# Experts sorted by the quarters of 64 tokens that pick them, and the V product summed in three phases

## The chip, the cores and the metric

The kernel runs on one core of a Trainium2 chip. The metric is the device time of one execution in microseconds; lower is better. The engines are named as in the profile: PE is TensorE (matrix products; PEld its weight loads), DVE is VectorE, ACT is ScalarE, POOL is GpSimd, SP is SyncE, which here only issues transfers.

## What is computed

One decoder layer over 256 tokens of width 2048: a mixer of two attention groups, and after it PEER, a retrieval over 128 x 128 single-neuron experts. Only PEER is touched here:

```python
def peer(xn, wq, subkeys, u, v):
    q = (xt @ wq).reshape(T, PEER_HEADS, 2, PEER_QDIM // 2)
    s1 = einsum('thd,nd->thn', q[:, :, 0], subkeys[0])      # 8 heads, 128 keys on either side
    s2 = einsum('thd,nd->thn', q[:, :, 1], subkeys[1])
    v1, i1 = top_k(s1, 16); v2, i2 = top_k(s2, 16)
    cand = v1[..., :, None] + v2[..., None, :]
    sc, ci = top_k(cand, 16)                                # 16 experts per head: 128 picks per token
    idx = i1[ci // 16] * 128 + i2[ci % 16]
    gate = softmax(sc)
    h = gelu(einsum('cd,chkd->chk', xc, u[ic]))             # xc, ic, gc: 128 tokens at a time
    return einsum('chk,chkd->cd', gc * h, v[ic])            # 16384 experts, rows of 2048
```

The result is `rmsnorm(h + peer(rmsnorm(h)))`, in float32.

## The kernel before

The kernel does not gather the experts of each token. It computes the hidden value of every expert for every token (the U stage), multiplies by the gates (zero where a token has not picked the expert), and multiplies the result A, experts x tokens, by V (the V stage). An expert that no token has picked adds nothing, so the V stage reads only picked experts, in tiles of 128 gathered rows.

**Marks.** While the picks are routed, matmuls of one-hot rows count them into `pc[t]`, one 128x128 table (expert = row and column) for each set `t` of 128 tokens. `used[:, t]` is 1 where a count is over 0.5. The last two columns of experts (`LATE = 2`) are left out of the lists: they are always multiplied, for both sets.

**Lists.** In the second part of the U stage, `todo` holds small steps, one after each `u_block` of 128 experts (`FETCH = 104` is the block by which all must be done). `alone` marks the experts that only set 0, or only set 1, has picked. For each of the two, `turned_sums` and `ranks` count (three small matmuls) the rank of each expert, and `keep` gives the first `128 * SINGLE` of them a place. The rest, those of both sets and those that did not fit, get places by `keep_rest`. `spots` and 16 `list_run`s turn places into the tables `idxA` and `idxV`, one column for each tile. So there are 27 + 27 tiles with a single set and 50 tiles with both, 104 in all (`LIST`); with the two late ones the V stage has 106. If the last list overflows, a branch at the end (`tc.If`) runs the other 102 tiles; it costs nothing otherwise.

**V stage.** `SEQ` is the order of the tiles: the two late ones, then a both-tile followed by one or two single ones, 48 times, then two both-tiles. For tile `n`:

- `gather_v` (line 1045, POOL) gathers 128 rows of V, 8 KB each, into one of 7 places of `ring`; it is called 6 tiles ahead.
- `gather_a` (line 1049, POOL) gathers 128 rows of `At` (256 tokens, 1 KB) into one of 3 buffers `ar`, 3 tiles ahead.
- `v_parts` (lines 1107 and 1108) splits each half of the V rows (128x1024) into a rounded part `hi` (ACT) and a remainder `lo` (DVE). There are four buffers of each, enough for two tiles.
- `a_parts` (lines 1096 and 1097) does the same with A: `ah` (ACT) and `al` (DVE), two buffers each. For a single tile only 128 tokens are split.
- `v_products` (lines 1143 to 1145) does three matmuls for each of four column blocks `c` of 512 and for each set `t` that the tile has: 12 for a single tile, 24 for a both-tile. They add into the eight PSUM banks `sums[t, c]`, from the first tile to the last. Six of the banks have the name `pv` in the profile, and the two with `t = 1, c > 1` are called `mm`.

The parts of tile `i + 1` are issued, with high priority, before the products of tile `i`. At the end `finish` (line 1152) adds a bank to `acc`, which holds the residual, and the last norm follows. The order of the instructions on each engine is set ahead of the run by the framework's scheduler, which follows priorities and its own estimate of when things are ready; on the chip every engine runs its list in order and waits on semaphores.

Of the kernel before, what the change touches and what calls it, by code (L numbers as in the profile page):

```python
# [10 lines left out]
F32 = mybir.dt.float32  # L11
F32R = mybir.dt.float32r
F16 = mybir.dt.float16
# [14 lines left out]
BIG = 3e38  # L28
RING = 7
LEAD = 13  # L30
SINGLE = 27
BOTH = 50
LIST = 2 * SINGLE + BOTH
LATE = 2
CAND = [16 // (i + 1) for i in range(16)]
NCAND = sum(CAND)
# [11 lines left out]
def decoder_trunk(ctx, tc, xT, g1, g2, gf, w_cols, w_v, w_out, w_q, u, v, subk, posk, posv,  # L48
# [4 lines left out]
    def f(ap):  # L53
        return ap.bitcast(F32)
# [561 lines left out]
    with ExitStack() as p3:  # L616
# [4 lines left out]
        used = qs0.bitcast(F16)[:, 0:256].rearrange("p (t c) -> p t c", t=2)  # L621

        HU = []

# [30 lines left out]
        with ExitStack() as pr:  # L655
            rt = pr.enter_context(tc.tile_pool(name="rt", bufs=1))
            ps4 = pr.enter_context(tc.tile_pool(name="ps4", bufs=1, space=bass.MemoryType.PSUM))

            pc = [ps4.tile([128, 128], F32, name=f"pc{t}") for t in range(2)]
# [44 lines left out]
            def route(t):  # L704
# [79 lines left out]
                def tok(t0):  # L784
                    if t0 % TG == 0:
                        st["stg"] = rt.tile([128, 128, TG], F32, name="stg", bufs=2)
                    stg = st["stg"]
                    r = t0 // RUN

                    hot = rt.tile([128, 2, RUN // 2, 128, 2], F16, name="hot", bufs=2)  # L790
                    o1 = rt.tile([128, 2, RUN // 2, 128, 2], F16, name="o1", bufs=2)
                    full = [128, RUN, 128, 2]
                    dve.tensor_tensor(hot.rearrange("p a b i j -> p (a b) i j"), iotar[:, None].to_broadcast(full),
                                      iT[:, r].rearrange("p a (b j) -> p (a b) j", j=2)[:, :, None, :].to_broadcast(full),
                                      op=OP.is_equal)
                    half = [128, RUN // 2, 128, 2]
                    for j in range(2):
                        g_ = gT[:, r, j].rearrange("p (b j) -> p b j", j=2)
                        dve.tensor_tensor(o1[:, j], hot[:, 0], g_[:, :, None, :].to_broadcast(half), op=OP.mult)

                    def later():

                        first = None
                        for k0 in range(RUN - 4, -1, -4):
                            pg = ps4.tile([128, 4, 128], F32, name="tp", bufs=4)
                            for k in range(3, -1, -1):
                                for j in (1, 0):
# [5 lines left out]
                                pe.matmul(pc[t], hot[:, 1, (k0 + k) // 2, :, k % 2], hot[:, 0, (k0 + k) // 2, :, k % 2],  # L813
                                          start=c % 128 == RUN - 1, stop=c % 128 == 128 - RUN)
# [46 lines left out]
                settle(1)  # L861
            settle()
            u_end()
            for t in range(2):
                dve.tensor_scalar(used[:, t], pc[t], 0.5, None, op0=OP.is_gt)
            dve.memset(used[:, :, NKEY - LATE:], 0.0)


# [49 lines left out]
        colsum = kp.tile([128, 3], F32, name="colsum")  # L918
        one = [kp.tile([128, 128], F16, name=f"one{t}") for t in range(2)]
        kept = [kp.tile([128, 128], F16, name=f"kept{t}") for t in range(2)]  # L920
        rest = kp.tile([128, 128], F16, name="rest")
        place = kp.tile([128, 128], F32, name="place")
        st2 = {}

        def scratch():
            return psl.tile([128, 512], F32, name="sl", bufs=2)
# [15 lines left out]
            dve.memset(row, 0.0)  # L942
            sp.dma_start(At[0].rearrange("(a b) -> a b", a=2), row[0:2])

        def alone():
            both = up.tile([128, 128], F16, name="both", tag="fT")
            dve.tensor_tensor(both, used[:, 0], used[:, 1], op=OP.mult)
            for t in range(2):
                dve.tensor_tensor(one[t], used[:, t], both, op=OP.subtract)

        def turned_sums(f_, k):
            ps = scratch()
# [14 lines left out]
        def keep(t):  # L967
            ps = ranks(one[t])
            dve.scalar_tensor_tensor(kept[t], ps, 128.0 * SINGLE, one[t], op0=OP.is_lt, op1=OP.mult)
            dst = place if t == 0 else up.tile([128, 128], F32, name="row", bufs=2)  # L970
            dve.scalar_tensor_tensor(dst, ps, 1.0 + 128 * SINGLE * t, kept[t], op0=OP.add, op1=OP.mult)
            if t:
                dve.tensor_tensor(place, place, dst, op=OP.add)

        def others():
            dve.tensor_tensor(rest, used[:, 0], used[:, 1], op=OP.max)
            for t in range(2):
                dve.tensor_tensor(rest, rest, kept[t], op=OP.subtract)

        def keep_rest():  # L980
            ps = ranks(rest)
            pe.matmul(ps_tot := scratch()[:, 0:2], st2["tot"], ones16[:, 0:2], start=True, stop=True)
            dve.tensor_copy(count, ps_tot[:, 0:1])
            dst = up.tile([128, 128], F32, name="row", bufs=2)
            dve.scalar_tensor_tensor(dst, ps, 1.0 + 256 * SINGLE, rest, op0=OP.add, op1=OP.mult)
# [33 lines left out]

        def indices(pool_, pl):  # L1020

            dve.tensor_copy(idxA, pl)
            row = pool_.tile([128, 128], F32, name="row", bufs=2)
            dve.tensor_scalar(row, pl, -1.0, 0.0, op0=OP.add, op1=OP.max)
            dve.tensor_copy(idxV, row)

        todo = [consts2, alone]
        for t in range(2):
            todo += [lambda t=t: turned_sums(one[t], t), lambda t=t: keep(t)]
        todo += [others, lambda: turned_sums(rest, 2), keep_rest, lambda: spots(up, place)]  # L1030
        pl = psl.tile([128, 128], F32, name="pl")
        owing = []
        for r in range(128 // RUN):
# [12 lines left out]

        def gather_a(n):
            AR[n] = kp.tile([128, T], F32, name="ar", bufs=3)
            pool.indirect_dma_start(AR[n], None, At, bass.IndirectOffsetOnAxis(ap=idxA[:, n:n + 1], axis=0))  # L1049


        SEQ, tiles_of = list(range(-LATE, 0)), {}
        for n in SEQ:
            tiles_of[n] = (0, 1)
        for n in range(LIST):
            tiles_of[n] = (0,) if n < SINGLE else (1,) if n < 2 * SINGLE else (0, 1)
        m = BOTH - 2
        for k in range(m):
            SEQ += [2 * SINGLE + k] + list(range(2 * SINGLE * k // m, 2 * SINGLE * (k + 1) // m))
        SEQ += [LIST - 2, LIST - 1]  # L1060

        weighed = 0
        FETCH = 104
# [26 lines left out]
        def a_parts(n):  # L1090
            ar = AR.pop(n) if n >= 0 else AL[4 + n]
            ah = kp.tile([128, T], F32R, name="ah", bufs=2)
            al = kp.tile([128, T], F32R, name="al", bufs=2)
            ts = tiles_of[n]
            s_ = slice(128 * ts[0], 128 * ts[-1] + 128)
            act.activation(ah[:, s_], ar[:, s_], AF.Copy)  # L1096
            dve.tensor_tensor(al[:, s_], ar[:, s_], f(ah[:, s_]), op=OP.subtract)  # L1097
            return ah, al

        def v_parts(n):  # L1100
# [21 lines left out]
        with ExitStack() as pv_:  # L1122
# [13 lines left out]
            ends = {t: [n for n in SEQ if t in tiles_of[n]] for t in range(2)}  # L1136

            def v_products(n, t, c, ah, al, vv):
                hi, lo = vv[c // 2]
                tl, cl = slice(128 * t, 128 * t + 128), slice(512 * (c % 2), 512 * (c % 2) + 512)  # L1140
                first, last = n == ends[t][0], n == ends[t][-1]
                ps = sums[t, c]
                pe.matmul(ps, ah[:, tl], hi[:, cl], start=first, stop=False)  # L1143
                pe.matmul(ps, ah[:, tl], lo[:, cl], start=False, stop=False)  # L1144
                pe.matmul(ps, al[:, tl], hi[:, cl], start=False, stop=last)  # L1145

            scaled = {}

# [26 lines left out]
            for i, n in enumerate(SEQ):  # L1175
# [148 lines left out]
```

## Time and profile before

| | |
|---|---|
| time, median of 3 runs | 1684.7 us (1684.11 to 1686.45) |
| the profiled execution | 1688.74 us, its span 1686.9 us |
| mean granted clock of PE | 0.994 |
| PE busy | 1665.2 us, 99% of the span |
| DVE, ACT, POOL busy | 1225.2, 931.8, 404.4 us |
| PE products of the V stage | 1230.1 to about 1672 us |
| DMA | 383.22 MB, mean 227 GB/s |

A row of the profile names the line, engine and operation, what it writes and reads by the program's names, and a time in ns or us. In the timeline, the first number is the start in us and the second how long it took; the bracket at the end tells how long the engine had been idle, and on whose end it waited. In a table of stretches, each engine has its busy time and its number of instructions, followed by PE's granted clock, the share of the time that the DMA engines were busy, and GB/s. Matmuls overlap in the pipeline, so a row's duration is longer than the distance from one to the next.

### The profile page before, as it was taken

Reading aid. Unit: us, or ns where it says so; the run is one execution under the profiler, and the core shown is the slowest. Engines: PE = TensorE matmul, PEld = TensorE weight load, DVE = VectorE, ACT = ScalarE, POOL = GpSimd, SP = SyncE. Lnnn points to the kernel's source line nnn. Section 1 sums busy time; section 2 is a strip of 40 time slices with the busy share of each in tenths; the row PEclk is TensorE's granted clock in tenths of the full one; section 3 lists DMA queues with packets and bytes.
Section 4 is the critical chain, followed back from the end, with each engine's and each line's share of the span. In section 5 each row is a group of like instructions: output and inputs, shape, how many; then the busy total and the mean of one; then the engine's idle time right before and its main releaser. Section 6 shows DMA issues by size and latency. Waiting matters only on the chain.

```text
span 1686.9 us, 29563 instructions
## 1 busy us (share of the span) xinstructions
PE 1665.2 (99%) x11304; PEld 1495.1 (89%) x11304; DVE 1225.2 (73%) x2209; ACT 931.8 (55%) x1515; POOL 404.4 (24%) x390
## 2 busy tenths in 40 slices
PE   9999999999999999999999999999999999999996
PEld 8998889999999999999888888888878888888885
DVE  7687876688999985776887776555556666666665
ACT  6587765543445565565444444444455555555555
POOL 0010111100042200000211212111155655556550
PEclk9999999999999999999999999999999999999998
DMA  8444434555555676567999757777577777877771
GB/s 305 167 145 132 132 117 163 176 174 170 171 169 174 216 242 211 194 233 242 345 355 331 240 200 268 264 237 237 180 264 282 284 295 281 296 283 284 288 278 62
DMA packets 136289, 383.22 MB, mean 227 GB/s; under 512 B 12008, under 2 KB 67404, under 8 KB 120140
## 3 DMA queue, kind: packets, MB, share of 16 engines
q1 hardware_dynamic: 116172, 258.55, 46.3%
q0 software_dynamic: 19968, 122.70, 19.5%
q8 instruction: 91, 1.49, 0.3%
q14 instruction: 58, 0.48, 0.1%
HBM read 345.77 MB, written 35.44 MB: 226 GB/s over the span
## 4 chain that ended last, share of the span: by engine, by line
PE 95%; DVE 3%; DMA 1%; ACT 1%; issue 0%; SPq 0%; DVEq 0%; ACTq 0%
PE mm L640 17%; PE mm L156 10%; PE mm L157 10%; PE mm L158 10%; PE mm L641 9%; PE pv L1143 7%; PE pv L1144 6%; PE pv L1145 6%; PE mm L1143 2%; PE mm L1144 2%; PE mm L1145 2%; PE mm L556 2%; PE mm L557 2%; PE mm L558 2%; PE tp L809 2%; PE av L528 1%
## 5 line engine op out<-in xcount | busy, mean ns | idle before, releaser
L107 ACT ACTIVATE hi<-raw 128x1024 fp32r<-128x1024 f32 (+1 forms) x370 | 389.8, 1056 | 408.1 <-PE mm L640 156.2
L108 DVE TENSOR_TENSOR lo<-raw,hi 128x1024 fp32r<-128x1024 f32 (+1 forms) x370 | 460.0, 1245 | 190.7 <-ACT hi L107 189.1
L640 PE MATMUL mm<-X,hi 128*128 128x512 f32 x1216 | 429.0, 395 | 0.5 <-DVE hg L649 0.5
L156 PE MATMUL mm<-X,hi 128*128 128x256 f32 x1424 | 409.9, 288 | 0.0
L158 PE MATMUL mm<-X,lo 128*128 128x256 f32 x1424 | 404.1, 284 | 0.0
L157 PE MATMUL mm<-X,hi 128*128 128x256 f32 x1424 | 404.0, 284 | 0.0
L1108 DVE TENSOR_TENSOR lo<-hg,hi 128x1024 fp32r<-128x1024 f32 x212 | 259.8, 1226 | 120.1 <-ACT hi L1107 115.1
L641 PE MATMUL mm<-X,lo 128*128 128x256 f32 x1216 | 339.5, 279 | 0.0
L1107 ACT ACTIVATE hi<-hg 128x1024 fp32r<-128x1024 f32 x212 | 224.3, 1059 | 114.3 <-PE pv L1145 108.4
L640 PEld LDWEIGHTS mm<-X,hi 128*128 128x128 f32 x1216 | 227.9, 187 | 53.8 <-PE sl L953 0.7
L156 PEld LDWEIGHTS mm<-X,hi 128*128 128x128 f32 x1424 | 271.3, 190 | 4.1 <-issue 3.9
L157 PEld LDWEIGHTS mm<-X,hi 128*128 128x128 f32 x1424 | 269.1, 189 | 0.5 <-issue 0.4
L158 PEld LDWEIGHTS mm<-X,lo 128*128 128x128 f32 x1424 | 268.6, 189 | 1.0 <-DVE lo L108 0.6
L641 PEld LDWEIGHTS mm<-X,lo 128*128 128x128 f32 x1216 | 227.9, 187 | 0.0
L1144 PE MATMUL pv<-lo,ah 128*128 128x512 f32 x474 | 180.5, 395 | 0.0
L1143 PE MATMUL pv<-hi,ah 128*128 128x512 f32 x474 | 172.2, 397 | 1.7 <-ACT ah L1096 1.7
L1145 PE MATMUL pv<-hi,al 128*128 128x512 f32 x474 | 160.9, 395 | 0.0
L1045 POOL DMA_INDIRECT hg<-in_v_dram,idxV x104 | 140.3, 1349 | 61.5 <-DVE lo L1108 36.6
L650 POOL TENSOR_TENSOR hg<-hg,rB 128x256 f32<-128x256 f32 x74 | 69.7, 942 | 347.1 <-DVE hg L649 347.1
L1049 POOL DMA_INDIRECT ar<-At,idxA x104 | 111.4, 1071 | 130.8 <-DVE al L1097 110.3
L1143 PEld LDWEIGHTS pv<-hi,ah 128*128 128x128 f32 x474 | 89.1, 188 | 23.8 <-ACT ah L1096 2.0
L1144 PEld LDWEIGHTS pv<-lo,ah 128*128 128x128 f32 x474 | 89.1, 188 | 21.3
(286 smaller groups left out, 2252.9 us busy)
## 6 DMA issues: line engine op xcount, KB each, us to landing
raw<-in_u_dram SPq DMA_DIRECT2D x256, 512.0 KB, 4.7
raw<-in_w_cols_dram SPq DMA_DIRECT2D x42, 512.0 KB, 4.0
raw<-in_w_out_dram SPq DMA_DIRECT2D x32, 512.0 KB, 4.0
raw<-in_w_q_dram SPq DMA_DIRECT2D x32, 512.0 KB, 3.8
gs<-stg SPq DMA_DIRECT2D x16, 1024.0 KB, 4.8
gt<-gs SPq DMA_DIRECT2D x16, 1024.0 KB, 10.8
At<-a SPq DMA_DIRECT2D x31, 512.0 KB, 6.6
tb<-bd SPq DMA_DIRECT2D x16, 256.0 KB, 3.5
```

The lines of the kernel that those rows point to most:

```text
L107: act.activation(hi[:, :n], raw[:, :n], AF.Copy)
L108: dve.tensor_tensor(lo[:, :n], raw[:, :n], f(hi[:, :n]), op=OP.subtract)
L156: pe.matmul(ps, hi[:, i, :], X[:, db, 0:T], start=db == 0, stop=False)
L157: pe.matmul(ps, hi[:, i, :], X[:, db, T:], start=False, stop=False)
L158: pe.matmul(ps, lo[:, i, :], X[:, db, 0:T], start=False, stop=db == DB - 1)
L640: pe.matmul(ps.rearrange("p a t -> p (a t)"), hi[:, i, :], X[:, db], start=db == 0, stop=False)
L641: pe.matmul(ps[:, 0], lo[:, i, :], X[:, db, 0:T], start=False, stop=db == DB - 1)
L1107: act.activation(hi, r_, AF.Copy)
L1108: dve.tensor_tensor(lo, r_, f(hi), op=OP.subtract)
L1143: pe.matmul(ps, ah[:, tl], hi[:, cl], start=first, stop=False)
L1144: pe.matmul(ps, ah[:, tl], lo[:, cl], start=False, stop=False)
L1145: pe.matmul(ps, al[:, tl], hi[:, cl], start=False, stop=last)
```

## The change

Tokens fall into four quarters of 64. The counts are kept by quarter, and every expert gets a code from 1 to 15, the sum of 1, 2, 4, 8 for the quarters that have picked it. Experts with quarters of one half alone are single as before (27 tiles each). Of those picked from both halves, the ones with exactly two quarters (codes 5, 10, 9, 6) get lists of their own, six tiles each. These experts are single in another order of the quarters: with the order 0, 2, 1, 3 the first set of 128 tokens is quarters 0 and 2, and with 0, 3, 2, 1 it is quarters 0 and 3. An entry of `KINDS` holds the phase, the set, the code (None for a half alone) and the number of tiles. The list for both sets has 26 tiles instead of 50; the number of tiles stays 104.

A PSUM bank has a fixed order of tokens in its 128 partitions, so the V stage runs in three phases, one for each order of `ORDERS`. At the end of the first two, `put` adds each bank to `acc`, in two pieces of 64 partitions, and the next phase starts its sums anew. `a_parts` takes the quarters in the phase's order; in the first two phases it splits a tile for both sets in two pieces. The tiles of the first two lists gather only the half row of `At` that they need. In phase 0 three single tiles go before each both-tile, in phase 1 a both-tile begins and four single ones go before each of the others, and in phase 2 three or four.

```diff
+ORDERS = ((0, 2, 1, 3), (0, 3, 2, 1), (0, 1, 2, 3))
+KINDS = ((2, 0, None, 27), (2, 1, None, 27), (0, 0, 5, 6), (0, 1, 10, 6), (1, 0, 9, 6), (1, 1, 6, 6))
-SINGLE = 27
-BOTH = 50
+HALVES = sum(k[3] for k in KINDS)
+BOTH = 26
...
-            for t in range(2):
-                dve.tensor_scalar(used[:, t], pc[t], 0.5, None, op0=OP.is_gt)
+            for q in range(4):
+                dve.tensor_scalar(used[:, q], pc[q // 2][:, q % 2], 0.5, 2.0 ** q, op0=OP.is_gt, op1=OP.mult)
...
+        def codes():
+            for t in range(2):
+                dve.tensor_tensor(used[:, 2 * t + 1], used[:, 2 * t], used[:, 2 * t + 1], op=OP.add)
+            dve.tensor_tensor(used[:, 0], used[:, 1], used[:, 3], op=OP.add)
+            dve.tensor_scalar(rest, used[:, 0], 0.5, None, op0=OP.is_gt)
+
+        def members(k):
+            one = kp.tile([128, 128], F16, name="one", bufs=2)
+            if KINDS[k][2] is None:
+                dve.scalar_tensor_tensor(one, used[:, 3 - 2 * KINDS[k][1]], 0.5, rest, op0=OP.is_lt, op1=OP.mult)
+            else:
+                dve.tensor_scalar(one, used[:, 0], float(KINDS[k][2]), None, op0=OP.is_equal)
+            st2["one"] = one
+            turned_sums(one, k)
...
+        def keep(k):
+            ps, one, cap = ranks(st2["one"]), st2["one"], KINDS[k][3]
+            kept = kp.tile([128, 128], F16, name="kept", bufs=2)
+            dve.scalar_tensor_tensor(kept, ps, 128.0 * cap, one, op0=OP.is_lt, op1=OP.mult)
+            dst = up.tile([128, 128], F32, name="row", bufs=2) if k else place
+            dve.scalar_tensor_tensor(dst, ps, 1.0 + 128 * FROM[k], kept, op0=OP.add, op1=OP.mult)
+            if k:
+                dve.tensor_tensor(place, place, dst, op=OP.add)
+            dve.tensor_tensor(rest, rest, kept, op=OP.subtract)
...
-            dve.tensor_copy(idxA, pl)
+            n = KINDS[0][3]
+            for t in range(2):
+                dve.tensor_scalar(idxA[:, n * t:n * t + n], pl[:, n * t:n * t + n], 2.0, float(t), op0=OP.mult, op1=OP.add)
+            dve.tensor_copy(idxA[:, 2 * n:], pl[:, 2 * n:])
...
+            if n < 2 * KINDS[0][3]:
+                src, dst = At.rearrange("r (t c) -> (r t) c", t=2), AR[n][:, 128 * sets[n][0]:128 * sets[n][0] + 128]
+            else:
+                src, dst = At, AR[n]
+            pool.indirect_dma_start(dst, None, src, bass.IndirectOffsetOnAxis(ap=idxA[:, n:n + 1], axis=0))
...
-        m = BOTH - 2
-        for k in range(m):
-            SEQ += [2 * SINGLE + k] + list(range(2 * SINGLE * k // m, 2 * SINGLE * (k + 1) // m))
-        SEQ += [LIST - 2, LIST - 1]
+        for ph, m in ((0, 4), (1, 4), (2, BOTH - 10)):
+            h, first = halves[ph], 1 if ph else 0
+            if first:
+                SEQ.append(full.pop(0))
+            m -= first
+            for k in range(m):
+                SEQ += h[len(h) * k // m:len(h) * (k + 1) // m] + [full.pop(0)]
+            if ph == 2:
+                SEQ += full
...
@@ in a_parts @@
+            order = ORDERS[phase[n]]
+            if order == tuple(range(4)):
+                s_ = slice(128 * sets[n][0], 128 * sets[n][-1] + 128)
+                views = [(ar[:, s_], ah[:, s_], al[:, s_])]
+            else:
+                views = []
+                quarters = [x_.rearrange("p (q c) -> p q c", q=4) for x_ in (ar, ah, al)]
+                for t in sets[n]:
+                    x, y = order[2 * t:2 * t + 2]
+                    two = slice(x, y + 1, y - x) if y > x else slice(x, y - 1 if y else None, y - x)
+                    views.append((quarters[0][:, two], quarters[1][:, 2 * t:2 * t + 2], quarters[2][:, 2 * t:2 * t + 2]))
...
+            def put(ph, t, c):
+                for k in range(2):
+                    q = ORDERS[ph][2 * t + k]
+                    s = acc[q // 2][64 * (q % 2):64 * (q % 2) + 64, 512 * c:512 * c + 512]
+                    dve.tensor_tensor(s, sums[t, c][64 * k:64 * k + 64], s, op=OP.add)
...
-                for t in tiles_of[n]:
+                for t in sets[n]:
                     for c in range(4):
                         v_products(n, t, c, ah, al, vv)
+                        if phase[n] < 2 and n == ends[phase[n], t][-1]:
+                            with tc.high_priority():
+                                put(phase[n], t, c)
```

More of the change, by code (lines that the diff above doesn't have):

```diff
@@ L30 @@
 LEAD = 13
-SINGLE = 27
-BOTH = 50
-LIST = 2 * SINGLE + BOTH
+ORDERS = ((0, 2, 1, 3), (0, 3, 2, 1), (0, 1, 2, 3))
+KINDS = ((2, 0, None, 27), (2, 1, None, 27), (0, 0, 5, 6), (0, 1, 10, 6), (1, 0, 9, 6), (1, 1, 6, 6))
+HALVES = sum(k[3] for k in KINDS)
+BOTH = 26
+LIST = HALVES + BOTH
 LATE = 2
@@ L620, in decoder_trunk @@
         HG = {}
-        used = qs0.bitcast(F16)[:, 0:256].rearrange("p (t c) -> p t c", t=2)
+        used = qs0.bitcast(F16).rearrange("p (q c) -> p q c", q=4)
         HU = []
@@ L657, in decoder_trunk @@
             ps4 = pr.enter_context(tc.tile_pool(name="ps4", bufs=1, space=bass.MemoryType.PSUM))
-            pc = [ps4.tile([128, 128], F32, name=f"pc{t}") for t in range(2)]
+            pc = [ps4.tile([128, 2, 128], F32, name=f"pc{t}") for t in range(2)]
             VI = rt.tile([128, 2, 2, PH, 2, 16], F32, name="VI", tag="hot", bufs=2)
@@ L812, in later @@
                                 c = t0 + k0 + k
-                                pe.matmul(pc[t], hot[:, 1, (k0 + k) // 2, :, k % 2], hot[:, 0, (k0 + k) // 2, :, k % 2],
-                                          start=c % 128 == RUN - 1, stop=c % 128 == 128 - RUN)
+                                pe.matmul(pc[t][:, c // 64 % 2], hot[:, 1, (k0 + k) // 2, :, k % 2],
+                                          hot[:, 0, (k0 + k) // 2, :, k % 2],
+                                          start=c % 64 == RUN - 1, stop=c % 64 == 64 - RUN)
                             w = t0 % TG + k0
@@ L917, in decoder_trunk @@
         over = kp.tile([128, 128], F32, name="over")
-        colsum = kp.tile([128, 3], F32, name="colsum")
-        one = [kp.tile([128, 128], F16, name=f"one{t}") for t in range(2)]
-        kept = [kp.tile([128, 128], F16, name=f"kept{t}") for t in range(2)]
+        colsum = kp.tile([128, 1 + len(KINDS)], F32, name="colsum")
         rest = kp.tile([128, 128], F16, name="rest")
@@ L923, in decoder_trunk @@
         st2 = {}
+        FROM = [sum(k[3] for k in KINDS[:i]) for i in range(len(KINDS))]
         def scratch():
@@ L943, in consts2 @@
             sp.dma_start(At[0].rearrange("(a b) -> a b", a=2), row[0:2])
-        def alone():
-            both = up.tile([128, 128], F16, name="both", tag="fT")
-            dve.tensor_tensor(both, used[:, 0], used[:, 1], op=OP.mult)
+        def codes():
             for t in range(2):
-                dve.tensor_tensor(one[t], used[:, t], both, op=OP.subtract)
+                dve.tensor_tensor(used[:, 2 * t + 1], used[:, 2 * t], used[:, 2 * t + 1], op=OP.add)
[9 more added lines that the diff above has]
+            turned_sums(one, k)
         def turned_sums(f_, k):
@@ L965, in ranks @@
             return ps[:, 0:128]
[L967 to L972, printed above, removed]
+        def keep(k):
[5 more added lines that the diff above has]
+            if k:
                 dve.tensor_tensor(place, place, dst, op=OP.add)
[L975 to L978, printed above, removed]
+            dve.tensor_tensor(rest, rest, kept, op=OP.subtract)
         def keep_rest():
@@ L984, in keep_rest @@
             dst = up.tile([128, 128], F32, name="row", bufs=2)
-            dve.scalar_tensor_tensor(dst, ps, 1.0 + 256 * SINGLE, rest, op0=OP.add, op1=OP.mult)
+            dve.scalar_tensor_tensor(dst, ps, 1.0 + 128 * HALVES, rest, op0=OP.add, op1=OP.mult)
             dve.tensor_tensor(place, place, dst, op=OP.add)
@@ L1025, in indices @@
             dve.tensor_copy(idxV, row)
[L1027 to L1030, printed above, removed]
+        todo = [consts2, codes]
+        for k in range(len(KINDS)):
+            todo += [lambda k=k: members(k), lambda k=k: keep(k)]
+        todo += [lambda: turned_sums(rest, len(KINDS)), keep_rest, lambda: spots(up, place)]
         pl = psl.tile([128, 128], F32, name="pl")
@@ L1048, in gather_a @@
             AR[n] = kp.tile([128, T], F32, name="ar", bufs=3)
[L1049 to L1056, printed above, removed]
-        m = BOTH - 2
-        for k in range(m):
-            SEQ += [2 * SINGLE + k] + list(range(2 * SINGLE * k // m, 2 * SINGLE * (k + 1) // m))
-        SEQ += [LIST - 2, LIST - 1]
+            if n < 2 * KINDS[0][3]:
[3 more added lines that the diff above has]
+            pool.indirect_dma_start(dst, None, src, bass.IndirectOffsetOnAxis(ap=idxA[:, n:n + 1], axis=0))
+        sets, phase, halves = {}, {}, {}
+        for k, (ph, st_, _, cap) in enumerate(KINDS):
+            for n in range(FROM[k], FROM[k] + cap):
+                sets[n], phase[n] = (st_,), ph
+        for n in list(range(HALVES, LIST)) + list(range(-LATE, 0)):
+            sets[n] = (0, 1)
+        for ph in range(3):
+            two = [[n for n in range(HALVES) if phase[n] == ph and sets[n] == (t,)] for t in range(2)]
+            halves[ph] = [n for pair in zip(*two) for n in pair]
+        SEQ, full = list(range(-LATE, 0)), list(range(HALVES, LIST))
+        for ph, m in ((0, 4), (1, 4), (2, BOTH - 10)):
[7 more added lines that the diff above has]
+                SEQ += full
+            for n in SEQ:
+                phase.setdefault(n, ph)
         weighed = 0
@@ L1093, in a_parts @@
             al = kp.tile([128, T], F32R, name="al", bufs=2)
[L1094 to L1097, printed above, removed]
+            order = ORDERS[phase[n]]
[9 more added lines that the diff above has]
+                    views.append((quarters[0][:, two], quarters[1][:, 2 * t:2 * t + 2], quarters[2][:, 2 * t:2 * t + 2]))
+            for r_, h_, _ in views:
+                act.activation(h_, r_, AF.Copy)
+            for r_, h_, l_ in views:
+                dve.tensor_tensor(l_, r_, f(h_), op=OP.subtract)
             return ah, al
@@ L1135, in decoder_trunk @@
             r = vp.tile([128, 2], F32, name="r")
-            ends = {t: [n for n in SEQ if t in tiles_of[n]] for t in range(2)}
+            ends = {(ph, t): [n for n in SEQ if t in sets[n] and phase[n] == ph] for ph in range(3) for t in range(2)}
             def v_products(n, t, c, ah, al, vv):
@@ L1140, in v_products @@
                 tl, cl = slice(128 * t, 128 * t + 128), slice(512 * (c % 2), 512 * (c % 2) + 512)
-                first, last = n == ends[t][0], n == ends[t][-1]
+                first, last = n == ends[phase[n], t][0], n == ends[phase[n], t][-1]
                 ps = sums[t, c]
```

## The prediction, made before the change was run

> **What bounds the kernel now.** I read the page's busy shares and its chain first, then the stretches of the last third, then the timeline of single engines there.
>
> ```profile
> span 1686.9 us, 29563 instructions
> PE 1665.2 (99%) x11304; PEld 1495.1 (89%) x11304; DVE 1225.2 (73%) x2209; ACT 931.8 (55%) x1515; POOL 404.4 (24%) x390
> PE 95%; DVE 3%; DMA 1%; ACT 1%; issue 0%; SPq 0%; DVEq 0%; ACTq 0%
> ...
> 1237.00:1664.00 427.00, 427.00 (x1832) 344.04 (x1831) 283.48 (x311) 247.08 (x310) 241.03 (x198) 1.00 0.74 275
> ...
> L1143 PE MATMUL pv<-hi,ah x474: 393/398/499, 1230.1 to 1668.2; 128*128 128x512 f32 x158
> L1143 PE MATMUL mm<-hi,ah x158: 393/398/398, 1233.0 to 1671.9; 128*128 128x512 f32 x158
> ```
>
> The chain is PE for 95% of the span. The stage that the change edits (V) runs from 1230.1 to about 1672.3. In the stretch 1237 to 1664 PE is busy all 427.00 us at granted clock 1.00 with 1832 matmuls: one each 427.00/1832 = 0.233 us. The 0.39 us of a single row is the length of one in a pipeline and not its price. L1143 has 474 + 158 = 632 matmuls, and L1144 and L1145 as many: 1896 x 0.2333 = 442 us, the whole stage. So here the time is the number of matmuls, as long as nothing else gets slower than PE.
>
> How much room the others have shows in a tile that only one token half needs (I call it H: 12 matmuls; a tile for both, F, has 24).
>
> ```profile
> 1403.79 0.40 PE L1143 MATMUL pv<-hi,ah 128*128 128x512 f32 x1
> ...
> 1406.59 0.40 PE L1143 MATMUL pv<-hi,ah 128*128 128x512 f32 x1
> ...
> 1305.76 0.31 ACT L1096 ACTIVATE ah<-ar 128x128 fp32r<-128x128 f32 x1 [1.51 <-PE mm L1144]
> 1306.11 1.06 ACT L1107 ACTIVATE hi<-hg 128x1024 fp32r<-128x1024 f32 x1
> 1307.39 1.06 ACT L1107 ACTIVATE hi<-hg 128x1024 fp32r<-128x1024 f32 x1 [0.21 <-PE pv L1145]
> 1308.56 0.42 ACT L1096 ACTIVATE ah<-ar 128x256 fp32r<-128x256 f32 x1
> ...
> 1307.21 2.50 DVE L1108 TENSOR_TENSOR lo<-hg,hi 128x1024 fp32r<-128x1024 f32 x2 [0.82 <-ACT hi L1107]
> 1309.62 0.42 DVE L1097 TENSOR_TENSOR al<-ar,ah 128x256 fp32r<-128x256 f32 x1
> 1309.96 2.54 DVE L1108 TENSOR_TENSOR lo<-hg,hi 128x1024 fp32r<-128x1024 f32 x2
> 1312.42 0.28 DVE L1097 TENSOR_TENSOR al<-ar,ah 128x128 fp32r<-128x128 f32 x1
> 1312.68 1.23 DVE L1108 TENSOR_TENSOR lo<-hg,hi 128x1024 fp32r<-128x1024 f32 x1
> ```
>
> From 1403.79 to 1406.59 an H tile takes PE 2.80 us (12 x 0.233), so F takes 5.60. The other rows are one of the few places where two H tiles follow each other: DVE splits one tile from 1309.96 to 1312.68, 2.72 us, without a gap, and PE did not wait. So against H, DVE needs 2.72 of 2.80 us (97%), against F half. ACT is under it (two of 1.06 and one of 0.31).
>
> **The change, part by part.** (1) Matmuls removed. Before: 54 H and 52 F (50 listed and 2 late), 54 + 104 = 158 half tiles. After: 27 + 27 + 4 x 6 = 78 H and 26 + 2 = 28 F, 78 + 56 = 134. It stays at 106 tiles, and 24 half tiles of 12 matmuls go: 288 x 0.2333 = **-67.2 us**, all on the chain while PE stays the bound.
>
> (2) Sums moved out twice (`put`), after phases 0 and 1: 2 x 8 banks x 2 DVE additions of 64x512 out of PSUM = 32. The nearest rows:
>
> ```profile
> L1152 DVE TENSOR_TENSOR acc<-pv,acc x6: 680/682/691, 1667.9 to 1671.5; 128x512 f32<-128x512 f32 x6
> L279 DVE TENSOR_TENSOR early<-row,pv x8: 346/354/358, 47.2 to 49.4; 64x120 f32<-64x120 f32 x8
> L1108 DVE TENSOR_TENSOR lo<-hg,hi x212: 1221/1226/1245, 1221.0 to 1662.8; 128x1024 fp32r<-128x1024 f32 x106
> ```
>
> 64 partitions with 120 columns cost 0.354 and 128 with 512 cost 0.682, so I price by columns: 0.68 each, 10.9 us a phase end. Each phase but the last ends on an F tile, and the next begins with one. Take PE's start of the old F as 0. DVE first splits the new F (two 1.23 us parts and `al` in two pieces of 0.29), done near 4.0. The first four banks are complete at 2.8, the others at 5.6. Four puts take 5.4 us, to 9.4, while the new F wants its fourth bank between 6.3 (four banks opened at once) and 7.7 (bank by bank): a wait of 1.7 to 3.1. The other four end at 14.9; by then the next F, late by 3.1, wants its last at 5.6 + 3.1 + 2.8 + 0.7 = 12.2: 2.7 more. So 5.8 us a boundary, **+11.6 us** for two. What queues behind these additions on DVE is the split of the H tile that follows; it would be ready near 16.2, before that F ends at 17, so I charge it nothing more. Were it put ahead of them it adds 2.46 a boundary. Bounds: 4 (DVE gets ahead, 2 each) and 18 (9 each). Nothing is given back later: the H tiles behind leave DVE 0.08 us each.
>
> (3) Longer runs of H. Before F and H mostly alternate; after, F stands behind three (phase 0), four (1) or 3.6 (2) H tiles on average. By the 2.72 us a run costs nothing; by the two `lo` taken alone (2.56 by another such pair) and 0.29 it is 2.85, 0.05 over, 78 x 0.05 = 3.9. I take **+3**, nearer the latter, as the buffers hold just two tiles. Upper end 3.0 us an H tile: 78 x 0.2 = 16; lower end 0.
>
> (4) The gathers stay at 104 of V and 104 of A; 54 of A now read half rows. Their pace:
>
> ```profile
> 1302.43 1.11 POOL L1049 DMA_INDIRECT ar<-At,idxA  x1 [0.30 <-issue]
> 1303.84 0.94 POOL L1045 DMA_INDIRECT hg<-in_v_dram,idxV  x1 [0.30 <-issue]
> 1308.70 1.82 POOL L1045 DMA_INDIRECT hg<-in_v_dram,idxV  x1 [1.09 <-DVE lo L1108]
> DMA to landing us min/median/max: 2.7/4.8/7.8
> L1097 DVE TENSOR_TENSOR al<-ar,ah x104: 284/293/427, 1236.0 to 1662.4; 128x128 fp32r<-128x128 f32 x54, 128x256 fp32r<-128x256 f32 x50
> ...
> 840.00:880.00 40.00, 40.00 (x261) 34.85 (x260) 35.34 (x38) 19.65 (x28) 7.57 (x8) 1.00 1.06 359
> 1300.00:1340.00 40.00, 40.00 (x173) 32.25 (x172) 27.12 (x30) 23.35 (x31) 24.58 (x20) 1.00 0.74 277
> ```
>
> A gather that starts in the middle of DVE's `lo` (1308.70) takes 1.82, one that starts while DVE is idle (1303.84) 0.94: it ends 0.94 after about the moment when DVE ends an instruction. With DVE full, each gather can start at the next end, one per `lo`, and a tile has two of each: POOL keeps pace. DVE pays nothing: all 212 `lo` take 1221 to 1245 ns, with a gather beside them or not. So the sum gets 0 from their meeting. [...] DMA: 277 GB/s at share 0.74, and 359 GB/s was reached at 840 to 880. The densest stretch, phase 1, needs the bytes of five tiles in 16.8 us instead of 5/2 x 8.4 = 21: 277 x 21/16.8 = 346. Tight, but it lasts 56 us, with seven tiles of ring; 0 us, upper end in the second rival.
>
> (5) The lists: seven rankings instead of three, over 50 instead of 43 blocks of the U stage, in its old 53 places. Four more times three 128x128 matmuls on PE, and about six small DVE instructions.
>
> ```profile
> 920.00:940.00 20.00, 2.19 (x32) 1.84 (x32) 1.00 0.67 238
> PEld mm L640 <- PE sl L953: 0.7, 1, 0.7
> PE mm L640 <- DVE hg L649: 0.5, 1, 0.5
> L969 DVE SCALAR_TENSOR_TENSOR kept<-sl,one x2: 278/281/284, 811.2 to 815.4; 128x128 f16<-128x128 f32 x2
> ```
>
> A list matmul (L1015) is at most 2.19/32 = 0.07 us: 12 x 0.07 = 0.8. The waits beside three rankings are 1.2 us; four more, 1.6. Together **+2** with rounding down, between 0 and 6 (24 DVE instructions of 0.28, if none were hidden; what hides them is DVE's free eighth, 35.34 busy of 40 at 840 to 880). Two more `used` rows and two instructions in `indices` lie there too.
>
> (6) `ah` and `al` in two pieces for both halves of F in phases 0 and 1: 2 x 0.31 instead of 0.42 on ACT, under an F tile. Only the first tile is bare, where PE waits:
>
> ```profile
> PE pv L1143 <- ACT ah L1096: 1.7, 1, 1.7
> ```
>
> **+0.3**, between 0 and 1.
>
> Sum: -67.2 + 11.6 + 3 + 2 + 0.3 = -50.3. The profiled execution took 1688.74 us (span 1686.9 and 1.84 around it): 1638.4. It is 4.0 above the median of the runs, 1684.7, so the median becomes **1634**.
>
> **Rivals.** First, the splits do not keep up: ACT waits for a buffer (the 0.21 before 1307.39), and `ah`, `hi`, `lo` in a row are 0.31 + 1.06 + 1.23 = 2.6 plus three handings-over of about 0.1, more than 2.80. At 3.0 to 3.2 us an H tile it costs 16 to 31 instead of 3: 1647 to 1662. For it: just-in-time already, DVE 97%. Against it: the pair of H at 1305 shows no wait of PE.
>
> Second, the loop of A. Only three `ar` buffers: `al` frees one, POOL gathers, it lands, `ah` and `al` read it. At the median landing 1.1 (wait) + 1.8 + 4.8 + 0.6 = 8.3 for three tiles, under the 8.4 of three H; at the maximal 7.8 it is 11.3, 3.8 a tile. Five tiles take 18.8 instead of 16.8, 21 times: +42, so 1676. Fuller DMA speaks for it, that 1.1 and 1.8 are the long cases against.
>
> Third, on the other side: POOL's gather blocks DVE as DVE blocks POOL. Then a tile costs DVE 2.72 + 2 x 0.94 = 4.6, over H's 2.80: 106 x 4.6 + 10.9 x 2 = 509 instead of 442, so **1752**. By 78 H tiles it eats the 50 us from (50/78 + 0.08)/2 = 0.36 us of blocking per gather on. Against it stand the constant `lo` durations. [...]
>
> Fourth, that the change does not do what it says: over 26 x 128 = 3328 experts in the last list the kernel runs 102 more tiles, each of 24 matmuls, 102 x 5.6 = 571 us. A count of the reference's own picks, by quarters, leaves 3143 for it, so this needs a miscount.
>
> Fifth, the puts hide: scheduling them between the splits costs 4, not 11.6, and runs 0: 1624.
>
> **How the numbers follow.** Forecast, the terms near their values (1628 to 1645): 0.56. Puts hidden (1620 to 1628): 0.14. Splits behind (1645 to 1664): 0.18. A's loop (1664 to 1681): 0.05. Blocking or overflow, slower: 0.05. Within 0.2% (3.4 us, about what these runs can tell from no change): 0.02. The range leaves out the two slow cases, the loop and the top of the splits: 1621 to 1655, its ends also -67.2 + 4 and -67.2 + 18 + 16 + 3.
>
> **What would show it.** L1143 with 402 and 134 matmuls; the stage some 392 us long; 32 additions on `acc` near 0.68; PE waiting on DVE at two places, 1231 + 67 = about 1298 and, 56 + 6 later, about 1360, some 6 us each; elsewhere PE full at 173 matmuls in 40 us. Waits of PE on `lo` in runs of H would show (3) wrong, waits of ACT on the `ar` transfer (4), `lo` rows longer than 1.25 the blocking. The prediction falls if an H tile takes over 3.1 us, or if the boundaries cost over 10 each.

## Result and the profile after

The changed kernel takes 1633.8 us (median of 4 runs, 1631.82 to 1637.11), the kernel before 1684.7 (4 runs, 1684.11 to 1686.45): a ratio of 0.9698, interval 0.968 to 0.9717, 50.9 us less. The forecast was 1634.

From the page of the changed kernel (engine, busy us, share of the span, instructions; then its matmul group):

```profile
span 1630.1 us, 29098 instructions
PE 1600.3 (98%) x11028; PEld 1436.3 (88%) x11028; DVE 1242.5 (76%) x2281; ACT 924.7 (57%) x1533; POOL 408.6 (25%) x390
...
L1186 PE MATMUL pv<-hi,ah x402: 388/398/628, 1226.5 to 1612.9; 128*128 128x512 f32 x134
```

`v_products` now stands at lines 1186 to 1188. It has 402 matmuls of this form instead of 474, as listed. PE is busy 64.9 us less in a span that is 56.8 us shorter: so PE now stands some 8 us more.

To compare profiles stage by stage I cut the span at the last gelu of the U stage (group `hg<-hg`, where "to" is the start of the last). Its rows, before and then after:

```profile
L653 ACT ACTIVATE hg<-hg x128: 397/403/433, 444.8 to 1231.8; 128x256 f32<-128x256 f32 x128
```
```profile
L658 ACT ACTIVATE hg<-hg x128: 397/402/427, 440.1 to 1228.4; 128x256 f32<-128x256 f32 x128
```

| us | before | after | difference |
|---|---|---|---|
| up to the first gelu (not touched) | 444.8 | 440.1 | -4.7 |
| first to last gelu (the lists are made here) | 787.0 | 788.3 | +1.3 |
| last gelu to the end of the span ("V" from here on) | 455.1 | 401.7 | -53.4 |

The first line differs from profile to profile by up to 5 us (440 to 445 in those taken here), with nothing changed in it; so below I compare V, and not spans. Had the 288 matmuls gone and nothing been added, V would be 455.1 - 67.2 = 387.9. It is 13.8 above that.

Where the 13.8 lie shows in the stretches of the changed kernel (start:end, length, then busy us and count of PE, PEld, DVE, ACT, POOL; granted clock, DMA share, GB/s):

```profile
1290.00:1310.00 20.00, 17.70 (x70) 12.27 (x70) 19.53 (x27) 8.46 (x12) 7.46 (x6) 1.00 0.47 176
1310.00:1340.00 30.00, 30.00 (x130) 24.09 (x129) 23.96 (x30) 19.57 (x29) 24.40 (x19) 1.00 0.97 362
1340.00:1390.00 50.00, 43.71 (x172) 32.47 (x171) 39.68 (x50) 26.12 (x35) 28.00 (x24) 0.97 0.72 266
...
1391.00:1601.00 210.00, 210.00 (x901) 169.20 (x900) 163.72 (x188) 144.50 (x187) 144.94 (x119) 1.00 0.85 316
```

Full rate is one matmul per 0.2331 us, and phase 2 (1391 to 1601) has it: 210.00/901 = 0.2331. In 1290 to 1310, 85.8 would fit and 70 were done: 3.7 us lost. In 1340 to 1390, 214.5 would fit and 172 were done: 9.9 lost. That is 13.6 of the 13.8. Both places hold the end of a phase.

What happens at an end is told by single engines. At the first, PE stands five times, always for `acc`, 2.30 us in all by the brackets (a stand costs more than its bracket, which counts from the end of an overlapping row). DVE and POOL at the first, of the changed kernel (start, duration; the bracket is how long the engine had waited, and for what):

```profile
1291.43 8.50 DVE L1195 TENSOR_TENSOR acc<-pv,acc 64x512 f32<-64x512 f32 x12
1299.86 1.21 DVE L1151 TENSOR_TENSOR lo<-hg,hi 128x1024 fp32r<-128x1024 f32 x1
1301.10 2.82 DVE L1195 TENSOR_TENSOR acc<-mm,acc 64x512 f32<-64x512 f32 x4
1303.95 0.29 DVE L1140 TENSOR_TENSOR al<-ar,ah 128x128 fp32r<-128x128 f32 x1
...
1304.51 1.69 POOL L1068 DMA_INDIRECT ar<-At,idxA  x1 [11.13 <-DVE al L1140]
```

Twelve additions, one `lo`, four additions, and only then `al`. The next gather of A needs the buffer that this `al` reads last, so POOL stands for 11.13 us, and the gathers of V are behind it in POOL's list. DMA falls to a share of 0.47 in this stretch. PE runs through after the first end all the same (130 matmuls in 1310 to 1340, where 128.7 fit). Around the second it does not (PE's five longest stands first):

```profile
1346.91 0.50 PE L1186 MATMUL pv<-hi,ah 128*128 128x512 f32 x1 [1.36 <-ACT ah L1138]
1357.88 0.50 PE L1186 MATMUL pv<-hi,ah 128*128 128x512 f32 x1 [1.61 <-DVE acc L1195]
1359.40 0.47 PE L1186 MATMUL pv<-hi,ah 128*128 128x512 f32 x1 [0.55 <-DVE acc L1195]
1366.84 0.73 PE L1187 MATMUL pv<-lo,ah 128*128 128x512 f32 x2 [0.88 <-DVE lo L1151]
1388.13 0.74 PE L1186 MATMUL pv<-hi,ah 128*128 128x512 f32 x2 [1.20 <-ACT ah L1138]
...
1356.44 7.08 DVE L1195 TENSOR_TENSOR acc<-pv,acc 64x512 f32<-64x512 f32 x10
...
1367.54 1.23 DVE L1151 TENSOR_TENSOR lo<-hg,hi 128x1024 fp32r<-128x1024 f32 x1
1368.68 0.28 DVE L1140 TENSOR_TENSOR al<-ar,ah 128x128 fp32r<-128x128 f32 x1
...
1369.04 1.88 POOL L1060 DMA_INDIRECT hg<-in_v_dram,idxV  x1 [11.43 <-DVE al L1140]
...
1375.94 0.42 ACT L1138 ACTIVATE ah<-ar 128x256 fp32r<-128x256 f32 x1 [1.21 <-DMA ar<-At,idxA]
1381.00 0.31 ACT L1138 ACTIVATE ah<-ar 128x128 fp32r<-128x128 f32 x1 [2.39 <-DMA ar<-At,idxA]
1387.77 0.31 ACT L1138 ACTIVATE ah<-ar 128x128 fp32r<-128x128 f32 x1 [2.53 <-DMA ar<-At,idxA]
```

POOL stands for 11.43 us, this time with a gather of V in front. The bracket names `al`, but that `al` ended only 0.08 us before; the `lo` ahead of it ended 0.27 before, the distance that POOL also kept from the `al` of the first end. So it was most likely this `lo`, which reads the place of the V rows last. Either way it is an instruction behind the additions. Afterwards ACT waits for gathers of A that started late, until 1388, some 19 us after POOL went on. The stand of 1.36 us at 1346 comes before the first addition of the second end (1353.76); that it belongs to `put` follows only from the next experiment, where it is gone, and by what path is not shown.

### The profile page after: what moved, and what is told of

Its sections match the earlier page's. It is cut to its first block, busy times and chain, and to the rows that moved or that the text cites. A ratio compares the mean times of both kernels' runs of the same rounds, so it can differ in the third digit from the quotient of the medians.

```text
span 1630.1 us, 29098 instructions
## 1 busy us (share of the span) xinstructions
PE 1600.3 (98%) x11028; PEld 1436.3 (88%) x11028; DVE 1242.5 (76%) x2281; ACT 924.7 (57%) x1533; POOL 408.6 (25%) x390
## 5 line engine op out<-in xcount | busy, mean ns | idle before, releaser
L1060 POOL DMA_INDIRECT hg<-in_v_dram,idxV x104 | 134.0, 1288 | 57.9 <-issue 25.1
L1187 PE MATMUL pv<-lo,ah 128*128 128x512 f32 x402 | 138.9, 396 | 0.9 <-DVE lo L1151 0.9
L1068 POOL DMA_INDIRECT ar<-At,idxA x104 | 119.2, 1146 | 76.9 <-DVE al L1140 47.9
L1188 PE MATMUL pv<-hi,al 128*128 128x512 f32 x402 | 136.4, 397 | 0.0
L1186 PE MATMUL pv<-hi,ah 128*128 128x512 f32 x402 | 124.7, 401 | 8.0 <-ACT ah L1138 4.7
L1186 PEld LDWEIGHTS pv<-hi,ah 128*128 128x128 f32 x402 | 76.0, 190 | 30.7 <-ACT ah L1138 7.7
L658 ACT ACTIVATE hg<-hg 128x256 f32<-128x256 f32 x128 | 52.3, 409 | 78.9 <-DVE hg L657 40.9
```

## Experiments

Theory: the 13.8 us are the work of `put` on DVE, and nothing else of the change costs in the V stage. Rivals: the longer runs of single tiles cost (3), or the gathers of A do (4). Each ratio is to the kernel before as measured on the same chip (1684.0, 1686.3 or 1685.9 us); V is read from one profile of each kernel.

### e1_no_put: the sums without `put`

```diff
-                        if phase[n] < 2 and n == ends[phase[n], t][-1]:
-                            with tc.high_priority():
-                                put(phase[n], t, c)
```

> The 32 additions at the two phase ends are left out (the sums of phases 0 and 1 are dropped; everything else, the phases and their fresh starts of the banks included, stays). Theory (the additions hold DVE, and PE and the gathers wait behind them): the matmuls missing from the 10 us stretches around the two ends are worth 4 + 11 us, some 2 of it ahead of the second end, so about 13 less than 1634: 1621. Rival A (what is lost there is the loop of the A gathers and the runs of single tiles): 1632 to 1635. Rival B (the fresh start of a phase itself costs): 1628 or more.

Measured: 1620.7 us, ratio to the kernel before 0.9615 (0.9599 to 0.9631). V is 387.5, beside the 387.9 that the matmuls alone would leave. Both ends now run through (214.5 fit in 50 us):

```profile
1290.00:1310.00 20.00, 20.00 (x87) 16.11 (x86) 13.87 (x18) 11.95 (x18) 11.99 (x11) 1.00 0.80 296
...
1340.00:1390.00 50.00, 50.00 (x216) 40.30 (x215) 38.21 (x44) 32.76 (x45) 33.78 (x30) 1.00 0.86 317
```

So the loss goes with `put`, and runs of single tiles and gathers cost nothing without it.

### e2_lists_only: the new lists, the old order

```diff
-        for ph, m in ((0, 4), (1, 4), (2, BOTH - 10)):
...
+        for n in range(2 * KINDS[0][3], LIST):
+            sets[n], phase[n] = (0, 1), 2
+        h, full = list(range(2 * KINDS[0][3])), list(range(2 * KINDS[0][3], LIST))
+        m = len(full) - 2
+        for k in range(m):
+            SEQ += [full[k]] + h[len(h) * k // m:len(h) * (k + 1) // m]
+        SEQ += full[-2:]
...
```

> The lists are built as in the changed kernel (quarters, seven rankings, half rows gathered), but the 24 new tiles are multiplied for both sets, in one phase and in the order of before: the same 1896 matmuls as before. Theory: the V stage is as before and the lists cost what the two profiles differ between the first block of the second U part and its last, 1.3 us, up to the 2 of the prediction: 1686 to 1687 beside 1684.7 for the kernel before. Rival (the lists stall PE in the U stage): over 1689. If half rows made the gathers cheaper in a way that counts: below 1684.

Measured: 1685.9, ratio 1.0009 (0.9999 to 1.002). The U part takes 788.2 us, as in the changed kernel, and V 455.1, as before. The lists cost 1.9 us by the medians (between nothing and 3.4 by the interval) and 1.2 by the stage; the gain hangs on the tiles in V alone.

### e3_ar4: a fourth buffer `ar`

```diff
-            AR[n] = kp.tile([128, T], F32, name="ar", bufs=3)
+            AR[n] = kp.tile([128, T], F32, name="ar", bufs=4)
...
-                if LATE <= i < len(SEQ) - 3:
-                    gather_a(SEQ[i + 3])
+                if LATE <= i < len(SEQ) - 4:
+                    gather_a(SEQ[i + 4])
```

> Four buffers for the gathered rows of A instead of three, gathered four tiles ahead. Theory (late A rows are a consequence of the phase ends: POOL stood behind DVE for 11 us at the second one): 1 to 3 us less, 1631 to 1633. Rival A (the loop of three buffers is what is lost): 8 us less or better, 1626 or lower. If nothing hangs on A: 1634.

Measured: 1632.1, ratio 0.9677 (0.9658 to 0.9696). V is 398.5: of the 13.8 us, 3.2 go. ACT then waits for no gather of A any more, yet 10.6 us are left, so the three buffers are not the main thing. As a time of the whole kernel it can't be told from 1633.8.

### e6_half_put: whole banks, half the additions

```diff
-                for k in range(2):
-                    q = ORDERS[ph][2 * t + k]
-                    s = acc[q // 2][64 * (q % 2):64 * (q % 2) + 64, 512 * c:512 * c + 512]
-                    dve.tensor_tensor(s, sums[t, c][64 * k:64 * k + 64], s, op=OP.add)
+                s = acc[t][:, 512 * c:512 * c + 512]
+                dve.tensor_tensor(s, sums[t, c], s, op=OP.add)
```

> Each bank is added to acc in one addition of 128 partitions instead of two of 64 (the quarters land on the wrong tokens): 16 additions instead of 32. Theory: DVE needs 5.4 instead of 10.9 us at each end; by the working of the prediction with half the price the waits at a boundary shrink from 5.8 to under 1, so most of what leaving them out gives comes: 1622 to 1625. If the loss goes in proportion: half of 13, 1627. Rival (it is not DVE's time that counts): 1632 to 1635.

Measured: 1617.8, ratio 0.9597 (0.9581 to 0.9614): better than any theory said. DVE, POOL and the two stretches, of this kernel:

```profile
1293.70 3.68 DVE L1193 TENSOR_TENSOR acc<-pv,acc 128x512 f32<-128x512 f32 x6
...
1300.18 1.69 POOL L1068 DMA_INDIRECT ar<-At,idxA  x1 [4.52 <-DVE al L1140]
...
1290.00:1310.00 20.00, 20.00 (x87) 16.14 (x86) 17.54 (x25) 11.86 (x17) 11.86 (x10) 1.00 0.77 280
1340.00:1390.00 50.00, 50.00 (x216) 40.30 (x215) 41.09 (x52) 32.18 (x43) 35.05 (x30) 1.00 0.87 323
```

An addition over 128 partitions takes no longer than one over 64 (0.68 us a row; six in 3.68 here, twelve in 8.50 there), so an end now costs DVE half: 8 x 0.68 = 5.4 us. V is 387.8, as without `put` at all. POOL's wait falls from 11.13 to 4.52, and PE stands at neither end. So 5.4 us at an end are free, and the cost begins somewhere between 5.4 and 10.9. (Between the two profiles, the part up to the first gelu makes the difference to e1: 442.4 us here and 445.1 there.)

### e8_double_put: twice the additions

```diff
                     dve.tensor_tensor(s, sums[t, c][64 * k:64 * k + 64], s, op=OP.add)
+                    dve.tensor_tensor(s, sums[t, c][64 * k:64 * k + 64], s, op=OP.add)
```

> Every addition of a bank is made twice (the sums of phases 0 and 1 count double): 21.8 us of DVE at a phase end instead of 10.9. Theory (nothing up to about 5.4 us, and beyond it at least 1 us for 1 us of DVE): by the slope between 5.4 and 10.9 us (14 us for two ends, 1.28) 28 us more, 1662; with slope 1, 1656. Rival (in proportion to the number of additions): 14 us more, 1648.

Measured: 1653.0, ratio 0.9805 (0.979 to 0.982). V is 420.4, 18.7 more than in the changed kernel, for 21.8 us more on DVE. With e1 and e6 this gives a curve. DVE's work at an end, and V above 387.5 (both ends together): 0 and 0; 5.4 and 0.3; 10.9 and 14.2; 21.8 and 32.9. It is flat up to 5.4 at least; from there to 10.9, and from 10.9 to 21.8, each us of DVE costs 1.3 and 0.86 us on average. The 1653.0 missed both numbers given: 1656 or more of the theory and 1648 of the rival, cost in proportion. What speaks against the rival is the other side: it expected 7 less for half the work, and 13.9 of 14.2 went. Part of the steep side may be the clock: PE stood for `acc` 26.4 us in all and up to 11.8 at once in this kernel, and the mean granted clock was 0.86 from 1290 to 1340 and 0.91 from 1340 to 1400.

### e5_act_put and e7_act_ar4: let ACT copy the sums out

ACT copies the pieces that stay on their partitions into `aside`, and DVE adds them under later both-tiles; e7 has four buffers `ar` besides.

```diff
...
+                stay = [k for k in range(2) if ORDERS[ph][2 * t + k] % 2 == k]
+                act.activation(aside[ph, c][p], sums[t, c][p], AF.Copy)
+                put(ph, t, c, [k for k in range(2) if k not in stay], sums[t, c])
+                owed.append((ph, t, c, stay, aside[ph, c]))
...
+                if n in inner and phase[n]:
+                    for _ in range(4 if phase[n] == 1 else 1):
+                        if owed:
+                            put(*owed.pop(0))
```

> The pieces of a bank that stay on their partitions (8 of the 16 in phase 0, all in phase 1) are copied out by ACT, 16 copies of about 0.63, and DVE adds them to acc later, under inner tiles for both sets; only the 8 pieces of phase 0 that change partitions are still added by DVE at once (5.4 us). Theory (what matters is how much of the additions stands on DVE between the last tile of a phase and the splits of the next; 5.4 us cost next to nothing): the 14 us of the two phase ends go, 1620. Rival A (ACT, 87% busy in runs of single tiles, becomes the one that is waited for): 1624 to 1630. Rival B (the 24 later additions, 16 us of DVE, cost in the runs what they saved at the ends): 1630 or more.

> The copies by ACT together with four buffers for A. Theory (the late A rows came from the phase ends alone): the same as the copies alone within 2 us, 1620. Rival (the loop of A costs something by itself in the fuller stretches): 3 us or more below them.

Measured: 1632.1, ratio 0.9686 (0.9669 to 0.9702), and 1631.6, ratio 0.9674 (0.9658 to 0.9689); V of e5 is 400.8. The gain did not come. The timeline of e5 shows why:

```profile
1295.29 0.69 DVE L1207 TENSOR_TENSOR acc<-pv,acc 64x512 f32<-64x512 f32 x1 [0.73 <-issue]
1295.90 0.68 DVE L1207 TENSOR_TENSOR acc<-aside,acc 64x512 f32<-64x512 f32 x1
1296.50 0.69 DVE L1207 TENSOR_TENSOR acc<-pv,acc 64x512 f32<-64x512 f32 x1
...
1306.01 0.95 POOL L1068 DMA_INDIRECT ar<-At,idxA  x1 [9.38 <-DVE al L1140]
```

The additions of `aside`, written further down in the program, stand between those out of PSUM: the scheduler took each as soon as its copy was there. DVE has as much to do at the end as before, and POOL waits 9.38 us. These two kernels did not move the work, so they say nothing about what moving it brings.

### e9_act_late and e9b_act_late_ar4: the same, held back

```diff
...
+                            with tc.issue_after(last_split[0].ins):
+                                put(*owed.pop(0))
...
```

`last_split` is the last `al` issued. e9b has four buffers `ar` besides.

> As the run with the copies by ACT, but each of the 24 later additions is held on DVE's queue behind the splits that are issued under an inner tile for both sets (in the run before, the schedule put 8 of them at once between the others at the first phase end, so that DVE stood there as long as ever). What stays at a phase end is 5.4 us of DVE in phase 0 and none in phase 1. Theory (only the DVE time at the phase ends counts): the 13 to 14 us go, 1620. Rival A (ACT's copies, 5 us at each end, delay the splits): 1624 to 1630. Rival B (the additions cost in the runs of single tiles what they saved): 1630 or more.

> The same with four buffers for A. Theory (with the phase ends gone nothing is left for the buffer to do): the same within 2 us, 1620. Rival (the loop of A costs something in the fuller stretches): 1617 or less.

Measured: e9 1621.8, ratio 0.9629 (0.9614 to 0.9644); e9b 1618.4, ratio 0.9605 (0.9591 to 0.962). V is 390.4 and 388.0. First end of e9b:

```profile
1292.23 2.61 DVE L1208 TENSOR_TENSOR acc<-pv,acc 64x512 f32<-64x512 f32 x4 [0.73 <-ACT aside L1199]
...
1298.77 0.94 POOL L1068 DMA_INDIRECT ar<-At,idxA  x1 [5.20 <-DVE al L1140]
...
1290.00:1320.00 30.00, 29.95 (x129) 23.78 (x128) 27.41 (x38) 21.69 (x33) 19.30 (x14) 1.00 0.74 266
```

DVE has only eight additions left there (5.4 us, what e6 showed to be free), POOL waits 5.20, and PE does 129 matmuls of 129. The same additions as in the changed kernel, 24 of the 32 done later out of copies by ACT, cost nothing at the ends. Three buffers are not quite enough for this: V of e9 is 2.4 us longer than that of e9b, against the theory of "the same within 2 us", and in e9 ACT waits 13.3 us for gathers of A, in e9b not at all. By the medians e9b is 15 us faster than the changed kernel and 67.6 faster than the one before on its chip (1685.9).

### e4_all_h and e10_all_h_ar4: what lies below the ends

To see how far single tiles can follow each other, these leave out one set of every both-tile but the two late ones and the last two, so that nearly all tiles are single (288 matmuls fewer). e10 has four buffers `ar`.

```diff
+        for k, n in enumerate([n for n in SEQ if n >= HALVES][:-2]):
+            sets[n] = (k % 2,)
```

> 24 of the 26 listed tiles for both sets are multiplied for one set only, in turn (the other half of their products is left out): 288 matmuls less, so phase 2 is one run of 70 single tiles. Theory (an H tile is held by PE alone, 2.80 us): 67 us less, 1567. If DMA gives out (1.11 MB in 2.80 us are 397 GB/s, the best stretches of 10 us have 386 to 394 at share 1.0): 2.85 to 3.0 us a tile, 1570 to 1582. If the splits or the loop of A give out first: 3.1 us or more a tile, over 1588.

> The run with 70 single tiles behind each other (half of the products of 24 tiles left out), with four buffers for A instead of three. With three it took 1644, and ACT and PE waited for the A rows. Theory (the loop of A is what such a run breaks on: freed by al, gathered, landed, read): a fourth buffer lets the tile come down from about 3.4 us towards 2.8 to 3.0, 1585 to 1615. Rival (DMA's rate, or the order that the schedule gives the splits): 1630 or more.

Measured: e4 1644.2, ratio 0.9754 (0.9736 to 0.9773); e10 1605.7, ratio 0.9525 (0.9508 to 0.9543). With 288 matmuls fewer than the changed kernel e4 takes longer: the theory (1567) failed, and the third case, over 1588, came. The stretch and two rows of the waits in it (us in total, times, longest), of e4 and then of e10:

```profile
1390.00:1590.00 200.00, 169.67 (x650) 125.81 (x649) 139.18 (x164) 120.34 (x164) 136.25 (x112) 0.94 0.85 316
...
PE pv L1188 <- ACT ah L1140: 28.3, 16, 3.5
ACT ah L1140 <- DMA ar<-At,idxA: 22.4, 17, 2.7
```
```profile
1390.00:1590.00 200.00, 177.16 (x729) 137.31 (x727) 153.97 (x184) 132.35 (x186) 125.13 (x110) 0.98 0.81 310
...
PE pv L1188 <- ACT ah L1140: 19.1, 11, 2.9
ACT ah L1140 <- DMA ar<-At,idxA: 8.5, 7, 2.5
```

A single tile takes 12 x 200/650 = 3.69 us in e4 and 12 x 200/729 = 3.29 in e10, instead of 2.80. One more buffer in the loop of A (gather, landing, `ah`, `al`, buffer free) wins 38.5 us. So the loop of A does limit runs of single tiles when no both-tile comes between, at a pace that the second rival put at 3.8 us; some of the pace is the granted clock, 0.94 and 0.98 in these stretches. In the changed kernel the both-tiles give it time to recover: V without `put` is at its floor. What holds e10 above 2.80 is not settled: PE waits for `ah`, and `ah` for DMA only in part.

## Why the prediction was right, by its own steps

**(1) Matmuls: right.** 288 fewer, 0.2331 us each where PE runs through, and with `put` gone V falls by 67.6 against the 67.2 forecast.

**(2) `put`: the right place, 11.6 forecast and 13.8 measured, and the nearness is partly luck.** The additions took 0.68 us as priced:

```profile
L1195 DVE TENSOR_TENSOR acc<-pv,acc x24: 682/689/696, 1291.4 to 1362.8; 64x512 f32<-64x512 f32 x24
```

The places were right too (about 1298 and 1360). Their sizes were not: 5.8 each was forecast, 3.7 and 9.9 came. The step priced one kind of wait, that of PE for a bank. By the brackets PE stood for `acc` 2.30 us at the first end and 2.16 at the second. At the first end such stands went with 3.7 us lost; at that rate both ends make some 7 us (an estimate), not 11.6. The rest is what the step left out: in the stretch of the second end PE stood 3.2 us for `ah` and 0.9 for `lo`, and the low clock (last section) cost 1.7. So one sentence of the step fell: "I charge it nothing more", of the splits queued behind the additions. It counted when PE reads their results and left out what they free: `al` a buffer of `ar`, `lo` the place of the V rows. POOL's next gather waits for one of them, with all other gathers behind it, and at the second end ACT waited for late gathers until 1388. Waits of ACT on the `ar` transfer, named as the sign that (4) is wrong, came here, but their cause is (2): the profile of e1, without `put`, has none of `ah`. The row of the waits in the changed kernel (us in total, times, longest):

```profile
ACT ah L1138 <- DMA ar<-At,idxA: 12.4, 9, 2.5
```

What the walk through PE's and DVE's starts did give is that half the work is free: with half the additions it has the first four banks clear at 4.0 + 2.7 = 6.7, wanted between 6.3 and 7.7, and all eight at 9.4, wanted from 9.1. That is a wait of at most 0.4 us, and e6 shows 0.3 for both ends.

**(3) Runs of single tiles: 3 forecast, 0 measured.** e1's V and its full rate in all three phases show it. The value by the back-to-back pair (2.72) was the right one, and I had leaned to the other.

**(4) Gathers: 0 forecast, and 0 in the ordinary course.** The loop of A is real, as e4 and e10 show, but the both-tiles cover it.

**(5) Lists: 2 forecast, 1.3 measured** by the stage; the twelve profiles of kernels with the new lists have 788.2 to 789.1 us there, beside 787.0 in the one before, so 1.2 to 2.1. **(6) First tile: 0.3 forecast, nothing measured:** PE stands 1.6 us for its `ah`, and 1.7 before.

V and the lists together make -53.4 + 1.3 = -52.1 between the two profiles, beside -50.9 in the medians and -50.3 in the forecast. The terms missed by +2.2 (`put`), -3 (runs) and -1 (lists and first tile), and these nearly cancel. The size of the gain was foreseen, since the matmuls make most of it; that the forecast hit within 1 us is luck.

**The rivals.** Splits behind: not seen outside an end. The loop of A: only after an end, in e9 by 2.4 us, and in e4 and e10. Overflow: not seen, the `v_products` rows are as listed. POOL blocking DVE: not seen, the `lo` rows keep their length with 208 gathers among them:

```profile
L1151 DVE TENSOR_TENSOR lo<-hg,hi x212: 1208/1224/1270, 1217.5 to 1606.1; 128x1024 fp32r<-128x1024 f32 x106
```

It is the gathers that differ: two that started in the middle of a `lo` (1304.51 and 1369.04) took 1.69 and 1.88 us, one that started during the additions out of PSUM (1356.68) 0.94. Puts hidden: not in the changed kernel; e9 comes to it with the help of ACT, at 1621.8, beside the 1624 named for it.

## What to carry to other kernels

In this kernel, work put on an engine that had a little room cost nothing up to the room (0.3 us for both ends together, with 5.4 us of additions at each) and about its whole length above it (1.3 and then 0.86 us for each us on DVE); so ask for the size of the burst and not only for the mean share, and shorten or spread the burst before touching anything else. When instructions queue on an engine, follow everything behind them until a buffer comes free: the transfer that this buffer lets start may be what is late next, long after the engine itself has caught up (here ACT waited for gathers until 1388, and the last addition ended at 1367.5). Look in the timeline whether work that was meant for later has really been placed later, before judging by its time whether moving it helps.

## What had not been expected of the hardware

A short stand of PE was followed by half the clock. Stretches of the changed kernel at its second end:

```profile
1356.00:1358.00 2.00, 0.39 (x3) 0.12 (x2) 1.92 (x4) 0.68 (x1) 0.94 (x1) 1.00 0.22 86
1358.00:1360.00 2.00, 1.45 (x5) 0.95 (x6) 1.94 (x4) 0.31 (x1) 0.00 (x0) 0.93 0.83 205
1360.00:1362.00 2.00, 2.00 (x6) 1.52 (x5) 1.96 (x3) 0.00 (x0) 0.00 (x0) 0.50 0.76 320
1362.00:1364.00 2.00, 2.00 (x7) 1.58 (x7) 1.92 (x4) 0.00 (x0) 0.00 (x0) 0.71 0.00 0
```

PE stood 1.61 us for `acc`, did three matmuls, stood 0.55 more, and the granted clock was 0.93 from 1358 to 1360, 0.50 to 1362 and 0.71 to 1364. By the mean clock that is 0.07 x 2 + 0.5 x 2 + 0.29 x 2 = 1.7 us of PE's time (an estimate), part of the 9.9 lost there. At the first end, where PE also stood 2.3 us in 20 but never over 0.69 at once, the clock stayed at 1.00. It also stayed at 1.00 behind the single stands of 1.36 us (from 1348 to 1350) and 1.20 us (from 1388 to 1392). What sets the fall is not shown here.

One price had been assumed from unlike rows and is now measured: over 64 partitions an addition takes what it takes over 128 (0.68 us both, e6), so the two pieces of a bank cost double.
